# GpSimd's two-tensor instructions over 256 columns, issued in pieces of 256

## The chip, the cores and the metric

The kernel runs on one core of one Trainium2 chip. The core has five engines that run side by side and wait for one another through semaphores. The profile calls them PE (TensorE: matrix multiplications, with PEld for its weight loads), DVE (VectorE), ACT (ScalarE), POOL (GpSimd) and SP (SyncE, which here issues every DMA). The metric is the time of one execution on the device in microseconds, and the number that counts is the median over runs.

## The reference

One step of a one-layer streaming encoder, on a prompt of 2048 tokens and a sample of 32 tokens that has a cache of 128 past tokens. The model is 1024 wide.

```python
def merge(oa, ob, subln_g, out_norm_b, w_out, lam_init):
    B, T = oa.shape[:2]
    oa = rmsnorm(oa, subln_g, SUBLN_EPS) * (1.0 - lam_init)
    ob = rmsnorm(ob.reshape(B, T, WIDTH_B), out_norm_b)
    return jnp.concatenate([oa.reshape(B, T, WIDTH_A), ob], axis=-1) @ w_out

def ffn_ple(h, p, g_mlp, w_up, w_down, w_ple_gate, w_ple_proj):
    c = rmsnorm(h, g_mlp)
    h = h + jnp.square(jax.nn.relu(c @ w_up)) @ w_down
    return h + jax.nn.sigmoid(h @ w_ple_gate) * (p @ w_ple_proj)

# reference(), for the prompt
qa, ka, va, qb, kb, vb = split_proj(rmsnorm(hp, g_attn[i]), w_in[i])
oa = diff_attn_prompt(qa, ka, va, t5_table, lam)
ob = band_attn_prompt(qb, kb, vb, band_table[i])
hp = hp + merge(oa, ob, subln_g[i], out_norm_b[i], w_out[i], lam_init)
hp = ffn_ple(hp, p_prompt[i], g_mlp[i], w_up[i], w_down[i], w_ple_gate[i], w_ple_proj[i])
...
y_prompt = rmsnorm(hp, g_final)
```

Group A is differential attention: four heads, two query and key maps of 64 each, values of 128, a softmax per map and the difference of the two with a learned weight, and a mask by chunks of 64. Group B is attention in a band of nine chunks, with eight heads of 64. The sample goes through the same steps with its cache. The keys and values are outputs as well.

## The kernel before

**Numbers in two halves.** All data are 32-bit floats. Each operand of a large product is split into a high part in the matmul's own format and a low part, the rest. `split` does this: the high part is a copy, made by ACT or by DVE, and the low part is `raw - hi`, a two-tensor subtraction that POOL makes in most places and DVE in some. `mm3` then issues three matmuls for each term: high by high, high by low, low by high. In the profile they are lines 168, 169 and 170; the copy on ACT is line 149, that on DVE line 151, and the subtraction line 153.

**Weights.** `wunit` loads a piece of 128 x 1024 weights into `wr` (two buffers), and splits it into `wh` on ACT and `wl` on POOL (three buffers each). There are 338 such units. The next load into a `wr` waits until ACT and POOL have read the old contents.

**Blocks and stages.** The prompt is cut into four blocks of 512 tokens; the last has the 32 sample tokens added (544), and its matmuls run in two parts of 272. `prep` normalises and transposes the input of a block: the four small steps of `rsqrt` (lines 179 to 182, on one column, on DVE) lead to a transpose `rp` on PE, and `aH`, `aL` are its split. `proj` makes queries, keys and values; `attn_a` and `attn_b` are the two attentions; `outproj` (result `hd`, sum of squares `sqacc`), `cnorm` (`cH`, `cL`, which wait for line 859 on DVE), `mlp_up` and `mlp_down` (`ups`, `dps`), `gate` (`gps`, `pps`, `sig`) and `final` follow. In `attn_a`, `rsqrt` works on 256 columns and on POOL. The stages of different blocks are woven: generators yield, and `weave` or `weave2` advances one beside another. From about 2430 us on, blocks 2 and 3 run the MLP together.

**Who sets the order.** The generators give each instruction a priority by the order in which they issue it. A scheduler then sets the final order of each engine's stream, by its own estimates of what instructions cost (`schedule_with_timeline_sim=True`). So an instruction that is cut in pieces can also move others. On the chip, each engine works through its own stream in that order and waits at semaphores.

**The lines that the change touches**: the subtraction in `split` (153), the sums of squares in `onorm` (795) and `outproj` (844), and two steps of `gate` on POOL (997, 1014), where `sig` is first the logarithm of the sigmoid and `h` takes the gated sum. POOL's other two-tensor instructions (lines 637, and 179, 180 and 182 in `attn_a`) have at most 256 columns and are left alone.

Of the kernel before, what the change touches and what calls it, by code (L numbers as in the profile page):

```python
# [12 lines left out]
F32 = mybir.dt.float32  # L13
F32R = mybir.dt.float32r
AF = mybir.ActivationFunctionType
ALU = mybir.AluOpType
# [60 lines left out]
JB = [(0, 1), (2, 3), (4, 5), (6, 7, 8)]  # L77
ONP = (28, 1, 6)
ONQ = (8, 1, 1)


def drain(gen):
# [4 lines left out]
def weave2(main, sides, at):  # L87
    n = 0
    for _ in main:
        for i, side in enumerate(sides):  # L90
            if n in (at[0] + i * at[1], at[0] + i * at[1] + at[2]):
                next(side, None)
        n += 1
    for side in sides:
        drain(side)
# [37 lines left out]
class Kern:  # L133
# [5 lines left out]
    def dma(self, dst, src):  # L139
# [3 lines left out]
            src = src.bitcast(F32)  # L143
        self.nc.sync.dma_start(dst, src)

    def split(self, hi, lo, raw, hi_eng="act", lo_eng="pool"):
        nc = self.nc
        if hi_eng == "act":
            nc.scalar.activation(hi, raw, AF.Copy)  # L149
        else:  # L150
            nc.vector.tensor_copy(hi, raw)
        eng = nc.gpsimd if lo_eng == "pool" else nc.vector
        eng.tensor_tensor(lo, raw, hi.bitcast(F32), op=ALU.subtract)  # L153

    def wunit(self, src, shape, hi_eng="act", lo_eng="pool"):
        nc = self.nc
# [628 lines left out]
    def onorm(self, b, wk, ps, tag, dst):  # L785
        nc = self.nc
        n, t0 = BN[b], 512 * b
        sq = wk.tile([P, BLK], F32, tag="acc", bufs=2, name="sqacc")[:, :n]
        for k in range(4, 8):
            raw = self.raw_o(wk, k, t0, n)  # L790
            if k == 4:
                nc.scalar.activation(sq, raw, AF.Square)
            else:
                nc.scalar.activation(raw, raw, AF.Square)
                nc.gpsimd.tensor_tensor(sq, sq, raw, op=ALU.add)
        yield from self.colnorm2(sq, b, 1.0 / 512, wk, ps, tag, dst, [])

    def oload(self, b, wk, up, out):
# [20 lines left out]
    def outproj(self, b, wk, oact, ps, acc):  # L819
        nc, a = self.nc, self.a  # L820
        n, t0 = BN[b], 512 * b
        W = a["w_out"][0]
        sq = wk.tile([P, BLK], F32, tag="acc", bufs=2, name="sqacc2")[:, :n]
        acc.append(sq)
        for d in range(8):
            wh, wl = self.wunit(W[:, P * d : P * d + P].rearrange("(k p) c -> p k c", p=P), [8, P])
            h = wk.tile([P, BLK], F32, tag="tmp", bufs=4, name="hd")[:, :n]
            self.dma(h, self.xT[:, d, t0 : t0 + n])
            for s0, sn in SUBS[b]:
                p = ps.tile([P, 512], F32, tag="mm", name="ops")[:, :sn]  # L830
                self.mm3(
                    p,
                    [
                        (wh[:, k], wl[:, k], oact[0][k][:, s0 : s0 + sn], oact[1][k][:, s0 : s0 + sn])
                        for k in range(8)
                    ],
                )
                nc.vector.tensor_tensor(h[:, s0 : s0 + sn], h[:, s0 : s0 + sn], p, op=ALU.add)
            if d == 0:
                nc.scalar.activation(sq, h, AF.Square)  # L840
            else:
                tmp = wk.tile([P, BLK], F32, tag="tmp", bufs=4, name="tmp")[:, :n]
                nc.scalar.activation(tmp, h, AF.Square)
                nc.gpsimd.tensor_tensor(sq, sq, tmp, op=ALU.add)
            self.dma(self.hS[:, d, t0 : t0 + n], h)
            yield

# [118 lines left out]
    def gate(self, b, h, up, act, md):  # L966
        nc, a = self.nc, self.a
        n, t0 = BN[b], 512 * b
        Wg, Wp = a["w_ple_gate"][0], a["w_ple_proj"][0]
        pT = [[up.tile([P, BLK], F32R, tag="u", name="pT") for _ in range(2)] for _ in range(2)]  # L970
        for i in range(2):
            for k in range(2):
                self.dma(pT[i][k][:, :n], self.pS[:, i, k, t0 : t0 + n])
        hH = act.tile([P, 8, act.aw], F32R, tag="act", name="hH")
        hL = act.tile([P, 8, act.aw], F32R, tag="act", name="hL")
        for k in range(8):
            self.split(hH[:, k, :n], hL[:, k, :n], h[:, k, :n], "act", "dve" if k % 2 else "pool")
        for dq in range(2):
            ph, pl = self.wunit(
                Wp[:, 512 * dq : 512 * dq + 512].rearrange("(k p) c -> p k c", p=P), [2, 512]  # L980
            )
            for d4 in range(4):
                d = 4 * dq + d4
                wh, wl = self.wunit(Wg[:, P * d : P * d + P].rearrange("(k p) c -> p k c", p=P), [8, P])
                for s0, sn in SUBS[b]:
                    pg = md.tile([P, 512], F32, tag="mm", name="gps")[:, :sn]
                    self.mm3(
                        pg,
                        [(wh[:, k], wl[:, k], hH[:, k, s0 : s0 + sn], hL[:, k, s0 : s0 + sn]) for k in range(8)],
                    )  # L990
                    sg = up.tile([P, BLK], F32, tag="u", name="sig")[:, :sn]
                    sm = up.tile([P, BLK], F32, tag="u", name="sm")[:, :sn]
                    nc.scalar.activation(sg, pg, AF.Abs)
                    nc.vector.tensor_scalar(sm, pg, 0.0, None, op0=ALU.min)
                    nc.scalar.activation(sg, sg, AF.Exp, scale=-1.0)
                    nc.scalar.activation(sg, sg, AF.Ln, bias=1.0)
                    nc.gpsimd.tensor_tensor(sg, sm, sg, op=ALU.subtract)
                    nc.scalar.activation(sg, sg, AF.Exp)
                    pq = md.tile([P, 512], F32, tag="mm", name="pps")[:, :sn]
                    self.mm3(  # L1000
                        pq,
                        [
                            (
                                ph[:, k, P * d4 : P * d4 + P],
                                pl[:, k, P * d4 : P * d4 + P],
                                pT[0][k][:, s0 : s0 + sn],
                                pT[1][k][:, s0 : s0 + sn],
                            )
                            for k in range(2)
                        ],  # L1010
                    )
                    nc.vector.tensor_tensor(sg, sg, pq, op=ALU.mult)
                    hv = h[:, d, s0 : s0 + sn]
                    nc.gpsimd.tensor_tensor(hv, hv, sg, op=ALU.add)
                yield

    def final(self, b, h, up, fk, mm, md=None):
# [56 lines left out]
    def run(self):  # L1074
        tc, nc, a = self.tc, self.nc, self.a
        with ExitStack() as top:
# [110 lines left out]
            for b in HALVES[0]:  # L1187
# [6 lines left out]
                if b == 0:  # L1194
                    next(m)
                    self.colnorm(acc[1][0], 1, 1.0 / D, wk, mm, "mm", self.rS)
                weave2(m, [self.onorm(i, wk, mm, "mm", self.rB) for i in HALVES[1]] if b == 0 else [], ONQ)
                if b == 0:
# [85 lines left out]
```

## Time and profile before

| | us |
|---|---|
| median of 3 runs | 3313.28 |
| lowest and highest of them | 3307.74, 3317.84 |
| the profiled execution | 3310.69 |
| its span, from the first to the last instruction | 3308.8 |
| mean granted PE clock in it | 0.975 of full |

The profile is of one execution. Busy time of an engine is the union of its instructions; a matmul's end is modelled, so that consecutive matmuls overlap in the rows. A group of instructions is shown as line, engine, operation, output<-inputs, shapes and count, then busy us and the mean ns of one, then the engine's idle time ahead of them and what ended it. A row in order of time starts with its start and length in us, merged over `xN` instructions; brackets hold the idle time of the engine before it and its releaser. A row of the waits has the engine, the tile and the line that waited, what it waited for, the total in us, the number of times and the longest. A row of windows gives a stretch, its length, the busy us of the five engines, the granted PE clock as a share of full speed, the share of the DMA engines and GB/s.

### The profile page before, as it was taken

To read this page: it belongs to the slowest core of one execution; us is meant where nothing else is said; L and a number is where in the kernel's file an instruction comes from. 1 tells how busy PE (TensorE), PEld (TensorE's weight loads), DVE (VectorE), ACT (ScalarE), POOL (GpSimd) and SP (SyncE) were. 2 spreads that over 40 slices of the span, in tenths; PEclk is the share of its full clock that TensorE was granted. 3 is DMA by queue.
4 is the path that set the end of the run, shared out by engine and by line. 5 is a ranking of instruction groups with operands and counts; after the bars stand their busy time and mean duration, and the time that the engine had idled before them with its cause. 6 is when DMAs were issued, how large, how long until landed. Compare 5 with 4: busy or idle time off the path is not lost. (4 is left out here: it accounts for less than half of the span.)

```text
span 3308.8 us, 50118 instructions
## 1 busy us (share of the span) xinstructions
PE 3096.1 (94%) x17881; PEld 2710.5 (82%) x17881; DVE 1669.4 (50%) x3952; ACT 1698.4 (51%) x3717; POOL 1468.8 (44%) x1083
## 2 busy tenths in 40 slices
PE   6988989999989999999899999989889999999998
PEld 6877778889977888777777877877779999999987
DVE  6117777454555545476765656656442232223335
ACT  4226666566665766666665656654442222222245
POOL 4335654432334433444544444565753333333365
PEclk9999899999999999999999999999999999999999
DMA  7488777686788654545655345347631111111123
GB/s 232 159 252 244 205 217 205 204 247 195 215 235 215 180 145 134 155 132 138 200 136 136 112 132 144 116 146 226 178 105 52 45 46 50 46 45 45 53 86 101
DMA packets 519073, 488.93 MB, mean 148 GB/s; under 512 B 37884, under 2 KB 414016, under 8 KB 518824
## 3 DMA queue, kind: packets, MB, share of 16 engines
q1 hardware_dynamic: 518824, 485.73, 50.8%
q8 instruction: 142, 2.33, 0.3%
q14 instruction: 107, 0.88, 0.1%
HBM read 379.06 MB, written 110.49 MB: 148 GB/s over the span
## 5 line engine op out<-in xcount | busy, mean ns | idle before, releaser
L153 POOL TENSOR_TENSOR wl<-wr,wh 128x1024 fp32r<-128x1024 f32 x338 | 820.0, 2427 | 1026.3 <-ACT wh L149 983.4
L949 DVE TENSOR_TENSOR h<-h,dps 128x512 f32<-128x512 f32 (+1 forms) x640 | 373.1, 585 | 584.6 <-PE dps L170 572.2
L149 ACT ACTIVATE wh<-wr 128x1024 fp32r<-128x1024 f32 x338 | 356.9, 1056 | 563.9 <-PE dps L169 278.4
L168 PE MATMUL dps<-uh,wh 128*128 128x512 f32 (+1 forms) x1280 | 459.7, 359 | 22.0 <-DVE h L949 16.7
L168 PE MATMUL ups<-cH,wh 128*128 128x512 f32 (+1 forms) x1280 | 452.0, 353 | 8.2 <-ACT relu L914 8.0
L170 PE MATMUL dps<-uh,wl 128*128 128x512 f32 (+1 forms) x1280 | 451.7, 353 | 0.0
L169 PE MATMUL ups<-cL,wh 128*128 128x512 f32 (+1 forms) x1280 | 451.5, 353 | 0.0
L169 PE MATMUL dps<-ul,wh 128*128 128x512 f32 (+1 forms) x1280 | 451.4, 353 | 0.0
L170 PE MATMUL ups<-cH,wl 128*128 128x512 f32 (+1 forms) x1280 | 451.0, 352 | 0.0
L168 PEld LDWEIGHTS dps<-uh,wh 128*128 128x128 f32 x1280 | 242.8, 190 | 57.0 <-DVE h L949 22.8
L168 PEld LDWEIGHTS ups<-cH,wh 128*128 128x128 f32 x1280 | 241.4, 189 | 40.9 <-ACT relu L914 8.6
L170 PEld LDWEIGHTS dps<-uh,wl 128*128 128x128 f32 x1280 | 241.7, 189 | 33.0
L169 PEld LDWEIGHTS ups<-cL,wh 128*128 128x128 f32 x1280 | 241.9, 189 | 31.1 <-DVE cL L153 0.4
L170 PEld LDWEIGHTS ups<-cH,wl 128*128 128x128 f32 x1280 | 241.7, 189 | 30.1
L153 POOL TENSOR_TENSOR ul<-relu,uh 128x272 fp32r<-128x272 f32 (+1 forms) x160 | 174.9, 1093 | 205.2 <-ACT uh L149 203.8
L169 PEld LDWEIGHTS dps<-ul,wh 128*128 128x128 f32 x1280 | 242.4, 189 | 26.3
L168 PE MATMUL qps<-aH,wh 128*128 128x512 f32 (+1 forms) x640 | 231.5, 362 | 6.8 <-ACT wh L149 3.4
L545 PE MATMUL s<-ka,q 128*128 128x256 f32 (+4 forms) x784 | 192.7, 348 | 40.8 <-issue 15.7
L169 PE MATMUL qps<-aL,wh 128*128 128x512 f32 (+1 forms) x640 | 229.8, 359 | 0.0
L170 PE MATMUL qps<-aH,wl 128*128 128x512 f32 (+1 forms) x640 | 229.3, 358 | 0.0
L559 ACT ACTIVATE e<-s,nm 128x512 f32<-128x512 f32 (+3 forms) x256 | 155.1, 610 | 94.7 <-DVE nm L551 70.9
L545 PEld LDWEIGHTS s<-ka,q 128*128 128x128 f32 (+1 forms) x784 | 135.7, 195 | 66.4 <-issue 27.9
(217 smaller groups left out, 7056.9 us busy)
## 6 DMA issues: line engine op xcount, KB each, us to landing
wr<-w_up SPq DMA_DIRECT2D x96, 512.0 KB, 4.2
wr<-w_down SPq DMA_DIRECT2D x96, 512.0 KB, 3.7
wr<-w_in SPq DMA_DIRECT2D x74, 512.0 KB, 5.2
q<-qS SPq DMA_DIRECT2D x256, 128.0 KB, 4.3
v<-vSa SPq DMA_DIRECT2D x64, 512.0 KB, 3.8
ka<-kS SPq DMA_DIRECT2D x32, 512.0 KB, 7.9
wr<-w_out SPq DMA_DIRECT2D x32, 512.0 KB, 5.0
wr<-w_ple_gate SPq DMA_DIRECT2D x32, 512.0 KB, 4.4
```

Of the source, the lines that this page charges most:

```text
L149: nc.scalar.activation(hi, raw, AF.Copy)
L153: eng.tensor_tensor(lo, raw, hi.bitcast(F32), op=ALU.subtract)
L168: nc.tensor.matmul(ps, lh, rh, start=start and i == 0, stop=False)
L169: nc.tensor.matmul(ps, lh, rl, start=False, stop=False)
L170: nc.tensor.matmul(ps, ll, rh, start=False, stop=stop and i == n - 1)
L545: nc.tensor.matmul(s, q[:, m, hl, P * qi : P * qi + nr], kt[:, m, k0 : k0 + n], start=hl == 0, stop=hl == 1)
L559: nc.scalar.activation(dst, src, AF.Exp, bias=nmx, accum_out=z[:nr, m, bi : bi + 1])
L949: nc.vector.tensor_tensor(hv, hv, ps, op=ALU.add)
```

## The change

A new method, `pool_tt`, takes the place of five two-tensor instructions on POOL. It issues the same operation in pieces of at most 256 columns: a flat operand in equal parts (1024 in four, 512 in two, 272 in two of 136, 544 in three), and one with two free dimensions by whole rows of it, or row by row where a row is wider than 256. What is computed is the same. The instructions of DVE, ACT, PE and the DMAs are the same in number and shape.

```diff
+PW = 256
...
+    def pool_tt(self, out, a, b, op):
+        nc = self.nc
+        if len(out.shape) == 2:
+            n = out.shape[1]
+            m = -(-n // PW)
+            for i in range(m):
+                sl = slice(n * i // m, n * (i + 1) // m)
+                nc.gpsimd.tensor_tensor(out[:, sl], a[:, sl], b[:, sl], op=op)
+            return
+        k, n = out.shape[1:]
+        if n > PW:
+            for i in range(k):
+                self.pool_tt(out[:, i], a[:, i], b[:, i], op)
+            return
+        s = PW // n
+        for i in range(0, k, s):
+            sl = slice(i, min(i + s, k))
+            nc.gpsimd.tensor_tensor(out[:, sl], a[:, sl], b[:, sl], op=op)
+
     def split(self, hi, lo, raw, hi_eng="act", lo_eng="pool"):
...
-        eng = nc.gpsimd if lo_eng == "pool" else nc.vector
-        eng.tensor_tensor(lo, raw, hi.bitcast(F32), op=ALU.subtract)
+        if lo_eng == "pool":
+            self.pool_tt(lo, raw, hi.bitcast(F32), ALU.subtract)
+        else:
+            nc.vector.tensor_tensor(lo, raw, hi.bitcast(F32), op=ALU.subtract)
...
-                nc.gpsimd.tensor_tensor(sq, sq, raw, op=ALU.add)
+                self.pool_tt(sq, sq, raw, ALU.add)
...
-                nc.gpsimd.tensor_tensor(sq, sq, tmp, op=ALU.add)
+                self.pool_tt(sq, sq, tmp, ALU.add)
...
-                    nc.gpsimd.tensor_tensor(sg, sm, sg, op=ALU.subtract)
+                    self.pool_tt(sg, sm, sg, ALU.subtract)
...
-                    nc.gpsimd.tensor_tensor(hv, hv, sg, op=ALU.add)
+                    self.pool_tt(hv, hv, sg, ALU.add)
```

## The prediction

> **What bounds the kernel now.** I read the page's busy shares first, then a table of six stretches, then PE's list of waits, and last the order of time around the longest of them. The first view is the page's head, and the table gives for each stretch its length, then busy us (and instructions) of PE, PEld, DVE, ACT and POOL, the granted PE clock, DMA share and GB/s.
>
> ```profile
> span 3308.8 us, 50118 instructions
> PE 3096.1 (94%) x17881; PEld 2710.5 (82%) x17881; DVE 1669.4 (50%) x3952; ACT 1698.4 (51%) x3717; POOL 1468.8 (44%) x1083
> ...
> 0.00:200.00 200.00, 173.05 (x994) 149.04 (x995) 73.33 (x156) 63.58 (x134) 81.88 (x58) 0.98 0.61 193
> 200.00:1100.00 900.00, 816.98 (x5124) 731.28 (x5123) 524.73 (x1563) 550.03 (x1312) 389.22 (x353) 0.95 0.79 224
> 1100.00:2150.00 1050.00, 998.84 (x5143) 841.35 (x5142) 642.16 (x1506) 658.79 (x1487) 471.46 (x331) 0.99 0.51 141
> 2150.00:2430.00 280.00, 246.81 (x1273) 208.43 (x1272) 155.02 (x196) 134.30 (x236) 188.18 (x113) 0.95 0.56 173
> 2430.00:3160.00 730.00, 728.46 (x4527) 660.86 (x4526) 212.56 (x417) 213.15 (x383) 246.49 (x164) 1.00 0.17 53
> 3160.00:3309.00 149.00, 131.97 (x828) 119.50 (x826) 61.55 (x115) 78.53 (x171) 91.56 (x69) 0.96 0.30 96
> ```
>
> PE sets the time nearly everywhere; POOL, which the change touches, is busy 44%. From 2430 to 3160 PE idles 1.5 us in 730, so nothing can be won there, and POOL at 34% leaves room. All that can move is PE's idle time elsewhere: 3308.8 - 3096.1 = 213 us, of which 83 lie in 200 to 1100, 51 in 1100 to 2150, 33 in 2150 to 2430, 27 in the first 200. These rows of PE's waits (total us, times, longest) say who ends them:
>
> ```profile
> PE rp L311 <- DVE rsy L182: 20.9, 7, 10.9
> PE dps L168 <- DVE h L949: 16.7, 14, 3.1
> ...
> PE sb L704 <- DVE stb L707: 15.7, 14, 4.4
> ...
> PE ups L168 <- ACT relu L914: 8.0, 1, 8.0
> PE gps L168 <- ACT wh L149: 7.5, 1, 7.5
> PE tpp L617 <- DVE e L582: 7.5, 8, 2.3
> ...
> PE vps L170 <- POOL aL L153: 2.1, 2, 1.8
> ...
> PE ops L170 <- POOL wl L153: 1.2, 2, 0.9
> ```
>
> DVE is named far more than POOL. So the question is what POOL's long instructions do to DVE.
>
> **The change part by part: more POOL work.** The rows of POOL with shapes kept apart (count, busy us, mean ns, idle before) that carry most of the count:
>
> ```profile
> L153 POOL TENSOR_TENSOR wl<-wr,wh 128x1024 fp32r<-128x1024 f32 x338 | 820.0, 2427 | 1026.3 <-ACT wh L149 983.4 <-ACT rsy L178 11.4 <-ACT pH L624 9.7
> L153 POOL TENSOR_TENSOR ul<-relu,uh 128x512 fp32r<-128x512 f32 x96 | 125.4, 1307 | 167.1 <-ACT uh L149 166.9
> L153 POOL TENSOR_TENSOR ul<-relu,uh 128x272 fp32r<-128x272 f32 x64 | 49.4, 773 | 38.1 <-ACT uh L149 36.9 <-DMA y_prompt<-yn 1.2
> ```
>
> A 1024-wide one becomes four, a 512 two, a 272 two of 136, a 544 three. The built programs hold 959 two-tensor instructions on POOL before and 2,391 after: 1,432 more, 338 x 3 + 96 + 64 = 1,174 of them in these rows. In nearly every case the pieces of one tile stand together, without a wait between them. Their price follows from POOL running back to back, in order of time, with a DVE row of the same moment:
>
> ```profile
> 2192.58 4.75 POOL L153 TENSOR_TENSOR wl<-wr,wh 128x1024 fp32r<-128x1024 f32 x2 [1.63 <-ACT wh L149]
> ...
> 2197.48 1.30 POOL L997 TENSOR_TENSOR sig<-sm,sig 128x512 f32<-128x512 f32 x1
> 2198.72 0.75 POOL L179 TENSOR_TENSOR rsv<-rsv,rsy 128x256 f32<-128x256 f32 x1
> 2199.42 0.27 POOL L153 TENSOR_TENSOR sl<-sq,sh 128x32 fp32r<-128x32 f32 x1
> ...
> 2197.56 1.25 DVE L151 CAST sh<-sq 128x32 fp32r<-128x32 f32 x1 [3.85 <-POOL sq L637]
> ```
>
> Two of 1024 take 4.75, so 2.37 each; a 256-wide one gives way to the next after 2199.42 - 2198.72 = 0.70. Four pieces are 2.80: 0.43 more for a whole unit, 0.14 for each added piece. 1,432 x 0.14 = 200 us of POOL, 44% to about 50% busy. Its cover is PE's own work, at 246 us of POOL under 730 of PE in the MLP and 188 under 280 in the densest stretch; without cover it would cost all 200. What shows now is POOL on PE's wait list (2.1 and 1.2 us and a few of about 1): some eight such waits, each 0.42 longer, +3 us (bounds 0 and +10, were the later wl passed on through ACT in the gates too). No DMA is added; wr, which both ACT and POOL read, comes free 0.4 us later under a transfer that waits on nothing else in the MLP.
>
> **What DVE gets.** The CAST above has 32 columns, yet it lasts 1.25 us: it starts 0.08 after POOL's sig and ends as that one ends. DVE instructions of this kind stand still while POOL runs one. In the first 32 us, rows of POOL, DVE and PE:
>
> ```profile
> 12.89 4.65 POOL L153 TENSOR_TENSOR wl<-wr,wh 128x1024 fp32r<-128x1024 f32 x2 [11.39 <-ACT rsy L178]
> ...
> 12.93 2.32 DVE L179 TENSOR_TENSOR rsv<-rsv,rsy 128x1 f32<-128x1 f32 x1 [0.70 <-ACT rsy L178]
> 15.29 2.27 DVE L180 TENSOR_TENSOR rsv<-rsv,rsy 128x1 f32<-128x1 f32 x1
> ...
> 18.91 1.94 PE L319 MATMUL xp<-ident,x 128*128 128x128 f32 x8 [5.68 <-issue]
> ...
> 26.72 2.36 DVE L179 TENSOR_TENSOR rsv<-rsv,rsy 128x1 f32<-128x1 f32 x1
> 29.11 2.27 DVE L180 TENSOR_TENSOR rsv<-rsv,rsy 128x1 f32<-128x1 f32 x1
> ...
> 31.82 0.32 PE L311 MATMUL rp<-ident,rsy 128*128 128x128 f32 x1 [2.33 <-DVE rsy L182]
> ```
>
> Instructions on one column wait out a whole wl twice running. Behind pieces each would wait at most 0.72: the first chain shortens by 4.59 - 1.44 = 3.1 of PE's 5.68, the second by 3.2, all of its 2.33. Together 5.4; I take -5 (bounds 0 and -8). The other clear place is the norm of blocks 2 and 3 (DVE, POOL and PE in order of time, the group row of DVE's L859, and a window):
>
> ```profile
> 2410.98 8.17 DVE L859 SCALAR_TENSOR_TENSOR tmp<-tmp,g_mlp_s,rl 128x544 f32<-128x544 f32 x4 [0.50 <-DMA tmp<-hS]
> ...
> 2411.07 5.72 POOL L153 TENSOR_TENSOR wl<-wr,wh 128x1024 fp32r<-128x1024 f32 x2
> ...
> 2421.63 0.59 PE L168 MATMUL ups<-cH,wh 128*128 128x272 f32 x1 [8.01 <-ACT relu L914]
> ...
> L859 DVE SCALAR_TENSOR_TENSOR tmp<-tmp,g_mlp_s,rl 128x544 f32<-128x544 f32 x8 | 15.8, 2023 | 0.5 <-DMA tmp<-hS 0.5
> ...
> 2376.98 0.77 DVE L859 SCALAR_TENSOR_TENSOR tmp<-tmp,g_mlp_s,rl 128x544 f32<-128x544 f32 x1
> ...
> 2416.00:2426.00 10.00, 4.37 (x19) 4.38 (x20) 7.32 (x5) 3.69 (x6) 8.58 (x6) 0.50 0.32 98
> ```
>
> L859 takes 0.77 when free and 2.02 on average. Four take 8.17; with at most 0.72 of waiting each they take 3.1 to 6.0, so 2.2 to 5.1 less. The same chain (tmp, cH on ACT, then wh behind it in ACT's queue) ends PE's wait of 7.5 us on wh in this stretch. I take 3 us from each wait, and 2 from the half-speed clock that follows: -8 (bounds 0 and -20, both waits and the clock gone). In return two wl took 5.72 here against 4.75: DVE gets in between POOL's instructions, and will between pieces.
>
> For 200 to 2150 I have only PE's rows: h 16.7, stb 15.7 and e 7.5, together 39.9 us in which DVE is late. These come after many things, PE itself among them; I take a fifth, -8 (bounds 0 and -40), half of it idle time and half the clock behind it. That such short waits cost clock is seen here, PE in time and a window:
>
> ```profile
> 717.88 0.31 PE L168 MATMUL vps<-wh,aH 128*32 128x256 f32 x1 [1.05 <-ACT vraw L361]
> ...
> 719.50:722.80 3.30, 3.22 (x14) 2.96 (x15) 2.21 (x13) 2.52 (x6) 0.85 (x4) 0.50 0.91 261
> ```
>
> A gap of 1.05 us is soon followed by 3.3 at half clock, some 1.7 us lost. The Trainium skill ("TensorE: Matmul & The Clock Gate", section "Why this matters for your kernels") asks only that gaps over about 3 us be avoided. By that rule the short gaps would carry no clock loss, the -8 would be -4, and the sum 4 us smaller, about 3303; the row disagrees, and I follow it.
>
> **What moves.** The two built programs keep PE's stages. In matmuls counted by place, the order of 2430 to 3160 is the same; between about 200 and 1100 and between 1700 and 2250 a matmul stands some 10 to 20 places from where it stood, 102 at most. DVE, ACT and SP shift alike. No row prices this. A gap newly opened costs 1 to 2 us and 1.7 of clock, and so does one closed; with four either way the bounds are -13 and +13. PE is busy nine tenths of the time there, so a shift uncovers a wait more easily than it covers one: +3. The end carries two 272-wide POOL steps, now two pieces each: +0.3.
>
> The sum: +3 - 5 - 8 - 8 + 3 + 0.3 = -14.7. The profiled execution took 3310.69 us (span 3308.8), 2.6 under the median of 3313.28, so 3296 for it and 3298.5 beside the median; I say 3299.
>
> **The rivals.** Hidden anyway: DVE's waits shrink but PE's gaps end on something else (a DMA, the next chain in ACT's queue), and -5 to -8 remain, eaten by +6: 3305 to 3320, say 3311. For it: only two places show the whole chain to PE. Against it: those two alone give 13.
>
> DVE does not get in: one row says so, in which a three-column instruction took longer than the longest of POOL's groups (2.43).
>
> ```profile
> 580.82 3.36 DVE L572 TENSOR_SCALAR c<-c,rz 128x3 f32<-128x3 f32 x1
> ```
>
> Were that the rule, DVE would wait 2.8 for four pieces, not 2.4, and the change would only cost: about 3316, counted with the hidden case. Against it stand the 5.72 for two wl and the L859 between them.
>
> POOL becomes the last in 2150 to 2430 (slower). It has 188 us there in 113 instructions; cut like the average, 113 x 1432/1083 = 149 more pieces add 21 us, to 209 of 280. If each new border let in a DVE instruction of 0.7 us, POOL would need 209 + 104 = 313, 33 over the stretch, and the weights would come late in every gate and output projection: up to 3346, about 3333 with half. It decides from (280 - 209) / 0.7 = 101 of 149 borders. Against it: DVE has 196 instructions in the stretch, and not all of them stop for POOL.
>
> The moved order (slower): in 200 to 1100 and 1700 to 2250, eight new gaps with their clock, 8 x 3.3 = 26, outweigh the -15 once five or six are opened on balance: about 3325.
>
> **How the numbers follow.** Forecast, faster: 0.48, own range 3280 to 3303. Hidden or not let in: 0.24. POOL last: 0.10. Moved order: 0.18. What a measurement can tell is about 0.3%, 9.9 us, so faster means under 3303.3 and slower over 3323.2: 0.48, 0.24 and 0.28. The range, 3270 to 3330, takes the forecast with all of its second bound in 2150 to 2430 and half of the one in 200 to 2150 at the low end, and the moved order and half of POOL's case at the high one.
>
> **What would show it.** POOL about 1,670 us busy, 2,515 instructions, pieces of wl near 0.75. DVE under 1,600, with L859 at 544 columns near 1.3 us and no L179 on one column over 1. PE's waits of 7.5 and 8.0 shorter, the 5.68 near 2.5; the stretch of 730 us unchanged. I am wrong if DVE's means stay, if PE's rows on POOL grow beyond 15 us, or if new gaps over 1 us stand between 200 and 1100 that no DVE row explains.

## The result, and the profile after

The changed kernel takes 3277.77 us (median of 4 runs, 3266.70 to 3285.98); the kernel before took 3313.89 beside it (4 runs, 3307.74 to 3317.84). The ratio is 0.9895, with a 95% interval of 0.987 to 0.992: 36 us faster by the medians, where 14.7 were forecast. A second set of runs of the same kernel, shown below as the last experiment, gave 0.9917 (0.9898 to 0.9935), so by the two intervals the gain is 21 to 43 us, with about 31 in the middle.

The profiled execution took 3282.74 us. First the head of its page, then the table of stretches that the prediction showed (length, busy us and instructions of PE, PEld, DVE, ACT and POOL, granted clock, DMA share, GB/s):

```profile
span 3281.0 us, 51609 instructions
PE 3096.6 (94%) x17881; PEld 2713.4 (83%) x17881; DVE 1562.2 (48%) x3952; ACT 1696.1 (52%) x3717; POOL 1711.0 (52%) x2515
...
200.00:1100.00 900.00, 829.23 (x5223) 741.49 (x5223) 494.64 (x1600) 562.32 (x1342) 453.78 (x684) 0.96 0.79 227
1100.00:2150.00 1050.00, 1008.27 (x5166) 850.89 (x5165) 616.05 (x1503) 662.57 (x1485) 559.68 (x793) 0.98 0.51 140
2150.00:2430.00 280.00, 247.38 (x1279) 210.91 (x1277) 130.99 (x181) 128.64 (x235) 213.46 (x288) 0.93 0.54 167
```

PE's busy time is what it was (3096.1 before), so the gain of this execution is PE's idle time: 212.7 before, 184.4 now, 28.3 less. DVE does the same 3,952 instructions in 107.2 us less, and POOL takes 242.2 more. Both engines are far from full; what changed is how long DVE's instructions stand. PE's waits on that (engine, tile and line, what it waited for, total us, times, longest):

```profile
PE rp L333 <- DVE rsy L204: 13.5, 5, 11.2
PE sb L726 <- DVE stb L729: 10.4, 13, 3.6
...
PE gps L190 <- ACT wh L169: 6.1, 1, 6.1
...
PE dps L190 <- DVE h L971: 5.5, 6, 1.6
PE ups L190 <- ACT relu L936: 5.0, 1, 5.0
...
PE ups L191 <- DVE cL L175: 3.6, 1, 3.6
...
PE tpp L639 <- DVE e L604: 2.6, 3, 1.2
...
PE ops L192 <- POOL wl L164: 1.4, 1, 1.4
```

The three rows from which the forecast took its largest unknown (h, stb and e, 39.9 us before) now hold 10.4 + 5.5 + 2.6 = 18.5. The wait of 7.5 us on wh is 6.1, that of 8.0 on relu is 5.0, and one of 3.6 on cL is new.

The groups of POOL and DVE, shapes kept apart (count, then busy us and the mean ns of one, then idle time before them). POOL after:

```profile
L164 POOL TENSOR_TENSOR wl<-wr,wh 128x256 fp32r<-128x256 f32 x936 | 690.9, 770 | 501.1 <-ACT wh L169 473.0 <-ACT rsy L200 11.7 <-PE tpb L741 6.6
L154 POOL TENSOR_TENSOR wl<-wr,wh 128x256 fp32r<-128x256 f32 x416 | 305.0, 764 | 407.0 <-ACT wh L169 403.7 <-ACT pH L646 3.2
```

DVE after:

```profile
L171 DVE CAST qh<-kr 128x512 fp32r<-128x512 f32 x24 | 12.9, 539 | 53.5 <-ACT kr L432 51.0 <-DMA pS<-pph 2.5
L175 DVE TENSOR_TENSOR cL<-tmp,cH 128x544 fp32r<-128x544 f32 x4 | 12.7, 3216 | 4.9 <-ACT cH L169 4.9
...
L201 DVE TENSOR_TENSOR rsv<-rsv,rsy 128x1 f32<-128x1 f32 x28 | 9.4, 335 | 16.0 <-ACT rsy L200 15.9
...
L881 DVE SCALAR_TENSOR_TENSOR tmp<-tmp,g_mlp_s,rl 128x544 f32<-128x544 f32 x8 | 7.8, 1025 | 6.1 <-DMA tmp<-hS 3.1 <-DMA rl<-rS 2.9
```

The same groups of DVE before, two rows that the prediction did not show:

```profile
L151 DVE CAST qh<-kr 128x512 fp32r<-128x512 f32 x24 | 31.7, 1322 | 50.6 <-ACT kr L410 43.9 <-issue 6.6
...
L151 DVE CAST qh<-kr 128x272 fp32r<-128x272 f32 x16 | 18.0, 1125 | 11.4 <-ACT kr L410 10.2 <-DMA kS<-qh 1.1
```

The cast of 512 columns took 1322 ns behind whole instructions, hardly more than the one of 272 columns, which is how a wait inside the duration shows itself. It takes 539 behind pieces, 24 times: 18.8 us less of DVE, in the middle of the chain that makes the queries and keys. The multiply on 544 columns went from 2023 to 1025. One row went the other way: the four cL of 544 columns now average 3216. That row is followed up below.

### The profile page after: what moved, and what is told of

It reads as the page before. It is cut to its first block, busy times and chain, and to the rows that moved or that the text cites. A ratio compares the mean times of both kernels' runs of the same rounds, so it can differ in the third digit from the quotient of the medians.

```text
span 3281.0 us, 51609 instructions
## 1 busy us (share of the span) xinstructions
PE 3096.6 (94%) x17881; PEld 2713.4 (83%) x17881; DVE 1562.2 (48%) x3952; ACT 1696.1 (52%) x3717; POOL 1711.0 (52%) x2515
## 3 DMA queue, kind: packets, MB, share of 16 engines
q8 instruction: 142, 2.33, 0.3%
## 4 chain that ended last, share of the span: by engine, by line
PE 54%; DMA 5%; DVE 4%; POOL 2%; ACT 1%; issue 1%; SPq 0%; DVEq 0%; POOLq 0%; ACTq 0%
PE dps L190 7%; PE ups L191 7%; PE ups L190 7%; PE ups L192 7%; PE dps L192 7%; PE dps L191 7%; PE s L567 2%; PE gps L190 1%; PE gps L191 1%; DMA ka<-kS 1%; PE gps L192 1%; PE tpp L639 1%; POOL wl L164 1%; DMA wr<-w_up 1%; PE ob L766 1%
## 5 line engine op out<-in xcount | busy, mean ns | idle before, releaser
L164 POOL TENSOR_TENSOR wl<-wr,wh 128x256 fp32r<-128x256 f32 x936 | 690.9, 770 | 501.1 <-ACT wh L169 473.0
L169 ACT ACTIVATE wh<-wr 128x1024 fp32r<-128x1024 f32 x338 | 356.9, 1056 | 581.0 <-PE dps L191 285.7
L154 POOL TENSOR_TENSOR wl<-wr,wh 128x256 fp32r<-128x256 f32 x416 | 305.0, 764 | 407.0 <-ACT wh L169 403.7
L154 POOL TENSOR_TENSOR ul<-relu,uh 128x136 fp32r<-128x136 f32 (+1 forms) x320 | 201.7, 652 | 167.7 <-ACT uh L169 166.4
L191 PEld LDWEIGHTS dps<-ul,wh 128*128 128x128 f32 x1280 | 242.2, 189 | 26.2
```

The source lines that it names most:

```text
L154: nc.gpsimd.tensor_tensor(out[:, sl], a[:, sl], b[:, sl], op=op)
L164: nc.gpsimd.tensor_tensor(out[:, sl], a[:, sl], b[:, sl], op=op)
L191: nc.tensor.matmul(ps, lh, rl, start=False, stop=False)
```

## The experiments

Most of these kernels hold every engine to the order of before, so that pieces and order can be told apart. This is done by order edges alone, from a table of the recorded order that is packed into the kernel; a cut instruction's pieces stand together at its old place. The table shifts the line numbers by up to 50 against the changed kernel (L154 is L204 there, L169 is L219).

```diff
+def ordered(tc, nc, cuts):
...
+        line = [i for k in rank for i in units[k]]
+        for before, after in zip(line, line[1:]):
+            tc.add_manual_dep(
+                after,
+                before.name,
+                mybir.DependencyInfo(mybir.DependencyClass.NoSync, mybir.DependencyReason.DATA),
+                reason="order",
+            )
...
+        ordered(tc, nc, k.cuts)
```

### Pieces and order, one at a time

The changed kernel's pieces in the order of before:

```diff
 PW = 256
...
+        ordered(tc, nc, k.cuts)
```

> The pieces of 256 columns, with PE, DVE, ACT, SP and POOL held to the order of the kernel before, tile by tile (order edges alone, no new waits). Theory of the lock (the pieces themselves pay, because DVE gets in sooner): most of the 36 us remains, ratio to before 0.988 to 0.993, DVE about 1,560 us busy, PE idle down by 20 us or more, most of it between 300 and 600 us and around 1,700. Theory of the order (the scheduler's other order pays): ratio 0.997 to 1.003, although DVE's busy time falls to about 1,560 all the same.

The kernel before, whole instructions, in the order of the changed kernel:

```diff
         eng = nc.gpsimd if lo_eng == "pool" else nc.vector
         eng.tensor_tensor(lo, raw, hi.bitcast(F32), op=ALU.subtract)
...
+        ordered(tc, nc, k.cuts)
```

> The whole instructions of the kernel before, with all five engines held to the order of the changed kernel (a cut instruction stands where its first piece stood). Theory of the lock: ratio 0.997 to 1.004, DVE back at about 1,670 us busy, PE idle about 210 us. Theory of the order: ratio 0.988 to 0.993 with DVE at 1,670. If both theories hold half each, this and the pieces in the old order are each near 0.995.

Measured: pieces alone 0.9884 (0.9869 to 0.9899), order alone 1.0047 (1.0035 to 1.0060), a little slower than the first theory allowed. The head of the page with pieces alone:

```profile
span 3273.8 us, 51633 instructions
PE 3091.8 (94%) x17881; PEld 2714.0 (83%) x17881; DVE 1552.1 (47%) x3952; ACT 1698.8 (52%) x3717; POOL 1706.7 (52%) x2515
```

The head of the page with the order alone:

```profile
span 3320.3 us, 50106 instructions
PE 3107.2 (94%) x17881; PEld 2715.6 (82%) x17881; DVE 1667.3 (50%) x3952; ACT 1696.4 (51%) x3717; POOL 1466.4 (44%) x1083
```

DVE is short with pieces in either order and long with whole instructions in either, so its lost time belongs to the length of POOL's instructions. To see where PE gains, each kernel's stretches are cut at the same matmul by count, so that each holds the same work. The row of the third stretch (columns as above) in the kernel before:

```profile
300.34:600.09 299.75, 260.14 (x1575) 232.10 (x1576) 220.55 (x600) 187.03 (x526) 168.75 (x158) 0.91 0.72 203
```

With pieces alone:

```profile
291.06:577.27 286.21, 256.75 (x1578) 230.44 (x1577) 194.00 (x600) 186.94 (x524) 186.62 (x265) 0.93 0.74 212
```

With the order alone:

```profile
314.17:593.21 279.04, 254.84 (x1577) 226.24 (x1577) 221.26 (x599) 185.26 (x523) 167.70 (x155) 0.94 0.77 217
```

With both, the changed kernel:

```profile
299.04:569.62 270.58, 251.15 (x1578) 224.34 (x1578) 200.57 (x599) 184.07 (x521) 187.82 (x266) 0.96 0.79 224
```

The lengths of all stretches, taken in the same way (us; the last column is the second look at the changed kernel):

| stretch, by before | before | pieces alone | order alone | both | both again |
|---|---|---|---|---|---|
| 0 to 100 | 100.1 | 94.5 | 105.9 | 97.9 | 96.0 |
| 100 to 300 | 200.3 | 196.6 | 208.2 | 201.2 | 202.4 |
| 300 to 600 | 299.8 | 286.2 | 279.0 | 270.6 | 266.9 |
| 600 to 1100 | 500.0 | 501.2 | 506.4 | 509.7 | 502.7 |
| 1100 to 1500 | 399.9 | 397.0 | 403.4 | 398.5 | 401.1 |
| 1500 to 1800 | 300.0 | 291.7 | 295.1 | 289.1 | 288.9 |
| 1800 to 2150 | 350.0 | 345.8 | 358.3 | 350.1 | 347.6 |
| 2150 to 2430 | 280.1 | 279.8 | 282.5 | 289.1 | 283.0 |
| 2430 to 3160 | 729.9 | 729.8 | 730.5 | 730.4 | 730.4 |
| 3160 to the end | 148.8 | 151.4 | 151.0 | 144.6 | 144.6 |

These lengths are of one execution each, and the two of the changed kernel differ by up to 7.0 us in a stretch, so differences of a few us in one stretch carry little.

Pieces alone win 5.6 us in the first 100 and 31.6 from 100 to 2150, in every stretch of it but one, and nothing behind. The order alone wins 20.7 in 300 to 600 and 4.9 in 1500 to 1800 and loses more than that elsewhere. So the 29.2 us that the changed kernel wins in 300 to 600 are more the order's than the pieces' (20.7 and 13.5 alone), and the order takes its share back in other places. Pieces pay; the moved order, over the whole kernel, does not.

### Is it DVE that gains, or PE's earlier start?

A rival remains: with pieces, PE can begin on the first part of a low half sooner. Here the pieces of each instruction are issued last columns first, old order:

```diff
-        for i in range(0, k, s):
+        for i in reversed(range(0, k, s)):
...
-            for i in range(m):
+            for i in reversed(range(m)):
```

> Pieces of 256 in the old order, but the pieces of each instruction are issued last columns first, so that the part which TensorE reads first is written last: no matmul can start earlier on a piece than it could behind the whole instruction. Theory (what pays is that VectorE gets in between pieces): as pieces first columns first, 0.986 to 0.991 of before, the sum of VectorE's waits for GpSimd near 130 us, TensorE 18 to 27 us ahead at 600 us. Rival (what pays is that TensorE, which waits for the low halves, may begin on the first piece): 0.997 to 1.003 and no lead at 600 us.

Measured: 0.9899 (0.9881 to 0.9916). The row of the third stretch ends at 580.64 where before's ends at 600.09, so PE is 19.4 us ahead there (22.8 with the pieces in the usual order):

```profile
293.58:580.64 287.06, 256.92 (x1575) 231.13 (x1576) 193.94 (x599) 186.18 (x523) 187.00 (x265) 0.92 0.74 212
```

PE's rows on POOL do grow (ops on wl 5.2 us where pieces in the usual order show 1.2), so the reversal does hold the matmuls back, and the gain stays. The rival falls.

### How small a piece

```diff
-PW = 256
+PW = 512
...
+        ordered(tc, nc, k.cuts)
```

> Pieces of at most 512 columns in the order of the kernel before: 372 more POOL instructions than before instead of 1,432. Theory of the lock: DVE waits behind at most 1.3 us, so between before and the pieces of 256: ratio 0.992 to 0.996, DVE near 1,610 us, POOL near 1,530. Theory of the order: 0.997 to 1.003.

The same with `PW = 128`:

> Pieces of at most 128 columns in the order of the kernel before: 3,545 more POOL instructions than before, at 0.14 us each some 500 us more POOL, near 2,000 busy (60%). Theory of the lock with POOL hidden: DVE near 1,530 us, ratio 0.985 to 0.992, no worse than pieces of 256. If the added POOL time comes through where POOL is densest (2,150 to 2,430 us): that stretch grows by 10 us or more and the ratio is 0.992 to 1.005. Theory of the order: 0.997 to 1.003.

And with 128, but 512 in the output projection, its norm and the gate (a `pw` argument at those nine calls):

```diff
-PW = 256
+PW = 128
...
-            wh, wl = self.wunit(W[:, P * d : P * d + P].rearrange("(k p) c -> p k c", p=P), [8, P])
+            wh, wl = self.wunit(W[:, P * d : P * d + P].rearrange("(k p) c -> p k c", p=P), [8, P], pw=512)
```

> Pieces of 128 everywhere but in the output projection, its norm and the gate, where they are 512; old order. Theory (128 lost because GpSimd's own time decides in 2150 to 2430 us and behind 3160 us, 33 us there): those stages go back to what pieces of 512 cost, so 0.988 to 0.994 of before, GpSimd near 1,880. Rival (128 is dear everywhere, by GpSimd's time or by VectorE locked out for longer): 1.000 to 1.008.

| pieces, old order | ratio | 95% interval | POOL busy us (instructions) | DVE busy us |
|---|---|---|---|---|
| whole (before) | 1 | | 1468.8 (1083) | 1669.4 |
| 512 | 0.9885 | 0.9870 to 0.9901 | 1533.3 (1455) | 1608.3 |
| 256 | 0.9884 | 0.9869 to 0.9899 | 1706.7 (2515) | 1552.1 |
| 128 | 1.0101 | 1.0087 to 1.0115 | 2022.8 (4628) | 1529.2 |
| 128, late 512 | 0.9934 | 0.9910 to 0.9957 | 1884.5 (3772) | 1542.0 |

DVE's time falls with each halving, PE's gain does not: 512 is as good as 256 (a smaller gain, 0.992 to 0.996, was expected), and 128 is 1% slower than whole, beyond every range stated for it. The two rows of the kernel with 128 that hold 2150 to 2430 say why:

```profile
2133.21:2293.75 160.54, 137.21 (x655) 112.81 (x653) 71.67 (x124) 73.84 (x143) 134.50 (x286) 0.95 0.52 165
2293.75:2439.95 146.20, 115.62 (x621) 98.40 (x620) 56.48 (x72) 59.83 (x95) 130.11 (x285) 0.91 0.48 149
```

POOL is busy 134.50 + 130.11 = 264.6 of 306.7 us, 86%, and the stretch is 26.7 us longer than before: POOL is the last there. ACT waits 69.5 us for POOL's sig in this stretch, 25.9 before. Coarse pieces in these stages alone bring the time down by 1.7%, so that is where most of the loss lay. It isn't all: with 128 early and 512 late the kernel is still 0.5% behind 256 everywhere. The stretch 300 to 600, where pieces of 256 win 13.5 us, takes 300.3 us with pieces of 128, as long as before. Whether POOL's own time or DVE locked out for longer does that, no run tells; the trace points to the second, since with 128 five DVE instructions of the whole kernel, three of them from 300 to 600, waited until 9 to 22 pieces had passed, and with 256 in the old order none waited for more than three.

### Which instructions

Only the low halves of the weights in pieces of 256, the rest whole; old order:

```diff
-PW = 256
+PW = 1 << 20
...
-            wh, wl = self.wunit(Wu[:, P * ft : P * ft + P].rearrange("(k p) c -> p k c", p=P), [8, P])
+            wh, wl = self.wunit(Wu[:, P * ft : P * ft + P].rearrange("(k p) c -> p k c", p=P), [8, P], pw=256)
```

> Only the low halves of the weight units (wl, 338 instructions of 1024 columns) are cut, in 1,352 pieces of 256; the 426 other two-tensor instructions of GpSimd that the change cuts stay whole; every engine has the order of before. Theory (a piece lets VectorE in, and the long instruction is what VectorE waits behind): the wl instructions of 2.4 us are 843 us of GpSimd's 1,466, so most of the 36 us of pieces in the old order comes: 0.9895 to 0.992 of before, GpSimd busy near 1,650. Rival (the gain comes from the short ones of 512 and 544 columns, ul, cL, hL, sig, h and the sums of squares, which sit in VectorE's own chains): 0.996 to 1.000.

The same argument at the two calls of the projections alone:

> Only the 74 weight units of the projections (before about 1,100 us) are cut in pieces of 256; the rest whole, old order. Theory (the gain lies where the profile after shows it, 17 to 29 us between 300 and 590 us): 0.991 to 0.995, matmuls ahead by 15 to 30 us at 600 us and nothing gained behind 1,100 us. Rival (the part before 1,100 us is only what the fuller queue of weights lets PE take early and is lost again later, so that it must be cut everywhere): 0.997 to 1.001.

Pieces of 256, but whole in the output projection, its norm and the gate (`pw=1 << 20` at those calls):

> Pieces of 256, but whole instructions in the output projection, its norm and the gate; old order. Theory (cutting gains nothing where GpSimd itself is last): 0.985 to 0.9885 of before, as good as pieces of 256 everywhere (0.9884) or up to 10 us better, since the 9.98 us in which VectorE stood behind 15 pieces cannot come there. Rival (in these stages too the cut lets VectorE in, the 7.5 and 8.0 us of waits in the norm of blocks 2 and 3 that the forecast named): 0.990 to 0.993.

Measured: all weights 0.9897 (0.9873 to 0.9921), projections 0.9954 (0.9938 to 0.9970), whole in the late stages 0.9886 (0.9865 to 0.9907). The weights carry the gain. Only PE reads wl, so no step of ACT that begins on a finished piece can be behind it. The 74 units of the projections alone carry 0.46 of the 1.16% of all pieces, just short of the theory's range. In 300 to 600 they do as much as all pieces:

```profile
297.18:583.20 286.02, 254.92 (x1576) 227.83 (x1577) 197.09 (x600) 186.84 (x524) 182.40 (x236) 0.93 0.74 213
```

Behind 1,100 us they win nothing more (their lead falls from 22 us there to 16 at the end). In the late stages pieces bring nothing that can be measured.

### The order that the scheduler makes

The change as it is, with 512 in place of 256:

```diff
-PW = 256
+PW = 512
```

> The change with pieces of 512 columns in place of 256, in the order that the scheduler makes of it. Theory (half the pieces let VectorE in as well, and the order that the scheduler makes moves the time by some 0.1 to 0.5%): 0.987 to 0.992. Rival (the order that comes of it decides): outside of that on either side, 0.993 to 1.000 or below 0.986.

The change with whole instructions in the late stages (`pw=1 << 20` at those calls, `PW = 256`):

> The change with whole instructions in the output projection, its norm and the gate, pieces of 256 elsewhere, in the order that the scheduler makes of it. Theory (the changed kernel loses about 7 us in 2150 to 2430 us because VectorE stood for 9.98 us behind 15 pieces in a row there): no wait of VectorE for GpSimd above 3.5 us in the norm, no loss in this stretch, 0.986 to 0.9885 of before. Rival (the loss comes from the moved order): again 4 us or more lost in that stretch and 0.989 to 0.992.

Measured: 0.9925 (0.9907 to 0.9944) and 0.9923 (0.9908 to 0.9938), both some 0.4% behind the same pieces in the old order (0.9885 and 0.9886). The first lies just outside the theory's range and short of the rival's. Neither beats the changed kernel, and those in the old order, 0.9884 to 0.9886, are not clear of it: the intervals overlap. The second was to show whether DVE's stand of 9.98 us cost the 9 us that the changed kernel loses in 2150 to 2430. The four cL of 544 columns do fall from a mean of 3216 ns to 1453, and the stretch takes 148.41 + 127.64 = 276.1 us, 4.0 less than before, where the changed kernel took 289.1:

```profile
2125.92:2274.33 148.41, 135.34 (x654) 112.17 (x653) 86.40 (x133) 76.74 (x153) 92.37 (x63) 0.95 0.56 174
2274.33:2401.97 127.64, 114.23 (x621) 99.37 (x620) 65.55 (x73) 61.16 (x96) 96.58 (x62) 0.93 0.56 173
```

The theory's range for the whole time was missed, since this order loses elsewhere. And of the 13.0 us between the two kernels in this stretch the stand can be only a part. The rows of the changed kernel:

```profile
2116.99:2273.83 156.84, 139.31 (x655) 114.88 (x654) 77.74 (x130) 74.97 (x147) 113.71 (x151) 0.92 0.54 170
2273.83:2406.07 132.24, 115.34 (x622) 100.28 (x620) 63.15 (x72) 59.94 (x95) 111.39 (x150) 0.91 0.54 165
```

Most of the loss is in the first row, ahead of the stand, where PE's busy time is 139.3 for the 134.5 of before at a clock of 0.92 for 0.97. The row of before:

```profile
2150.02:2300.02 150.00, 134.45 (x654) 110.53 (x653) 83.95 (x124) 73.44 (x141) 93.60 (x61) 0.97 0.56 175
```

The last run asked whether this belongs to the kernel or to one execution. Nothing is edited:

> The changed kernel once more, nothing edited. Theory (the 9.98 us in which VectorE stood behind 15 pieces and the half-speed clock in 2150 to 2430 us belong to one execution, not to the kernel): no low half cL of 544 columns above 3 us on VectorE, the matmuls that took 289.1 us from 2117.0 to 2406.1 us take 282 or less. Rival (its order brings it about each time): again a cL above 6 us, and 286 to 292 us. In either case 0.987 to 0.992 of before.

Measured: 0.9917 (0.9898 to 0.9935). The stand is there again, 15 pieces long (shown in the last section), so it belongs to the order. The stretch took 283.0 us, between what the two theories said: of the 9.0 us lost to before in the first profile 6.1 did not come again, 3.7 of them PE's busy time (137.3 + 113.6 = 250.9 against 254.6).

## Why the prediction was right in direction and short in size

**POOL's price: right.** Forecast 1,670 us and 2,515 instructions; 1,711.0 and 2,515. Where DVE gets nothing in between, 8 pieces of wl take 5.59 us (last section), 0.70 each, as priced. The other 40 us would be pieces that gave way to DVE, which was not counted. PE's waits on POOL stayed small, as forecast.

**The first 100 us, -5: right for the pieces.** Pieces alone won 5.6 there, the reversed ones 2.8. In the changed kernel its own order took some of that back (97.9 and 96.0 against 94.5). In order of time, DVE's one-column chain and PE's gap behind it:

```profile
13.25 0.70 DVE L201 TENSOR_TENSOR rsv<-rsv,rsy 128x1 f32<-128x1 f32 x1 [0.70 <-ACT rsy L200]
13.98 0.65 DVE L202 TENSOR_TENSOR rsv<-rsv,rsy 128x1 f32<-128x1 f32 x1
...
15.98 1.94 PE L341 MATMUL xp<-ident,x 128*128 128x128 f32 x8 [2.43 <-ACT rb L335]
```

Two instructions of 2.3 us became 0.70 and 0.65, each behind one piece, and PE's 5.68 became 2.43, where 2.5 was forecast. No instruction of this kind on 128 partitions takes more than 0.71 now. PE's second wait of 2.33 is gone with pieces alone, as forecast; in the changed kernel 0.98 of it is left.

**The norm of blocks 2 and 3, -8: wrong in sum.** The two waits shrank by 1.4 and 3.0 us where 3 each were forecast, and the multiply on 544 columns fell to 1.03 where 1.3 was. But pieces alone won 0.3 us in 2150 to 2430, and the changed kernel lost 9.0 and 2.9 there. The step had counted the waits that get shorter and not what takes their place: with the old order PE now waits 3.3 us on POOL's cL, with the new one 3.6 on DVE's.

**200 to 2150, -8: the term that was mis-sized.** Pieces alone won 31.6 from 100 to 2150 (bounds were 0 and -40). PE's rows with pieces alone:

```profile
PE sb L776 <- DVE stb L779: 15.9, 13, 4.9
...
PE dps L240 <- DVE h L1021: 4.6, 9, 1.3
PE tpp L689 <- DVE e L654: 3.7, 3, 1.9
```

Of the 39.9 us in these three rows 15.7 went, two fifths, where I took a fifth; the row on stb did not move, and it shrank only together with the order (21.4 in the changed kernel). The other part was in rows that the forecast left out: all of PE's waits on DVE from 100 to 2150 come to 57.6 us before and 35.0 with pieces alone, 22.6 of the 25.7 us of idle time won there. So PE's rows named the right engine, and the step failed in the share that it took of them. DVE's own groups by shape were not asked: there the cast of qh stood at 1322 ns, and the whole of DVE fell by 107 us.

Half of this term was to be clock. It was less, but not nothing. Over the same matmuls, from 100 to 2150 of before, PE is busy 1915.75 us before, 1909.83 with pieces alone, 1909.89 and 1901.38 in the two profiles of the changed kernel: 6 to 14 of the 31 to 40 us won there are PE's busy time, where a faster clock shows, and the rest is idle time. For the whole kernel the first profile shows nothing of it (3096.1 before, 3096.6 after), the second look does (3084.1). The granted clock averages 0.975 in 36 executions of before and 0.977 in 8 of the changed kernel; by an estimate from these, at most some 7 us of the gain are clock.

**The moved order, +3: right in sign, and small by cancelling.** Alone it costs 0.47%, 16 us, of the 26 that the rival allowed; it wins 20.7 in one stretch and gives more back. With pieces it costs 0.1 to 0.3% (0.9895 and 0.9917 against 0.9884).

**The whole.** The forecast's own range was 3280 to 3303, and 3277.77 lies just below it. It lies in the range of 3270 to 3330, whose low end had room for the middle (half its second bound) and for the norm; the norm gave none of it and the middle more than its share, so that the sum still fell inside is in part luck.

**The rivals.** Hidden anyway falls with the runs of pieces alone. POOL last does not come with 256 and does with 128, in the stretch named. But it is mostly POOL's own price there and not DVE let in at the borders: 16 pieces of wl take 6.73 us, 0.42 each, so the 571 pieces of the two rows above account for up to 240 of the 264.6 us by this estimate. Half of that rival's 33 us would also have been 3330, not 3333. DVE not let in is not the rule, but it occurs, and some small instructions do wait longer: the mean of `c<-c,rz,nlam` on 3 columns went from 304 to 434 ns. The price of 0.72 us at most per instruction held for most, not for all.

The Trainium skill ("SBUF — State Buffer", section "SBUF: two separate sides") says that a GpSimd instruction and a VectorE one in a two-port mode or with two inputs in SBUF take a shared port pair as an exclusive lock: whichever starts first has it for its whole instruction, and the other is blocked. The rows agree: the one-column instruction above, which has two inputs in SBUF, takes 0.70 behind a 256-column piece, and took 2.32 behind a 1024-column one.

## What to carry to other kernels

Where a long GpSimd instruction runs beside VectorE, compare each VectorE group's mean with its free time, shape by shape, beside TensorE's list of waits. Here a fifth of three rows of that list was far too little, and VectorE's sum was only a loose bound: 512 won as much with 61 us less of VectorE as 256 with 117. Two pieces of 512 gave all that four of 256 did here, at a quarter of the extra GpSimd time (64.5 us for 238 in the old order), and 128 lost it again where GpSimd was nearly full. Test such a change in the old instruction order too: here the order that the scheduler made of it took back 0.1 to 0.4% of a gain of 1.15%.

## What the runs showed of the hardware that was not expected

**A waiting DVE instruction is not always next.** POOL and DVE of the changed kernel in order of time, first profile:

```profile
2376.05 1.47 POOL L154 TENSOR_TENSOR sig<-sm,sig 128x256 f32<-128x256 f32 x2
2377.45 3.31 POOL L154 TENSOR_TENSOR cL<-tmp,cH 128x181 fp32r<-128x181 f32 x6
2380.67 5.59 POOL L164 TENSOR_TENSOR wl<-wr,wh 128x256 fp32r<-128x256 f32 x8
...
2376.86 10.62 DVE L175 TENSOR_TENSOR cL<-tmp,cH 128x544 fp32r<-128x544 f32 x2 [4.94 <-ACT cH L169]
```

The same in the second look:

```profile
2360.22 1.48 POOL L154 TENSOR_TENSOR sig<-sm,sig 128x256 f32<-128x256 f32 x2
2361.61 3.31 POOL L154 TENSOR_TENSOR cL<-tmp,cH 128x181 fp32r<-128x181 f32 x6
2364.84 5.59 POOL L164 TENSOR_TENSOR wl<-wr,wh 128x256 fp32r<-128x256 f32 x8
...
2361.44 10.20 DVE L175 TENSOR_TENSOR cL<-tmp,cH 128x544 fp32r<-128x544 f32 x2 [5.35 <-ACT cH L169]
```

The first of the two DVE instructions took 9.98 us in the first profile: it stood while the running piece of sig and 14 more went by, and ended only when POOL paused (for 5.74 us). With pieces of 128 one stood for 9.63 us at 2377.97. Elsewhere in the changed kernel DVE got in after one piece or two, but for one instruction that waited for five. What decides it is open: the trace doesn't show who asks for the port.

**Half clock after short gaps.** The granted clock of the kernel before falls to half in 30 episodes, nearly all 3.41 us long or a multiple of it (168 us in all), of the changed one in 30 (170 us). In 20 of the 30, in both, no gap of PE that reached into the 6 us before was as long as 3 us. One of these in the changed kernel, with PE's gap in order of time:

```profile
2129.42 0.39 PE L653 MATMUL o<-pH,v 128*128 128x256 f32 x1 [1.74 <-ACT pH L646]
```

The window behind it:

```profile
2129.90:2136.72 6.82, 5.83 (x14) 4.57 (x15) 2.78 (x7) 2.04 (x5) 4.44 (x7) 0.50 0.25 83
```

This speaks against the rule weighed in the prediction (the Trainium skill, "TensorE: Matmul & The Clock Gate", "Why this matters for your kernels"), which asks only that gaps over about 3 us be avoided. Less idle time did not mean fewer episodes in the first profile; the second look has 26 of them (134 us). So the change wins at most a little clock, as estimated above.
